# Seventeen of twenty-two up-projection pairs by half products, their weight sums spread over the kernel

## The chip, the cores and the metric

The kernel runs on one core of one Trainium2 chip, as one program in one launch. The metric is the time on the device in microseconds (us); lower is better. Engines are named as the profile names them: PE is the matrix engine (PEld its weight loads), DVE the vector engine, ACT the scalar engine, POOL GpSimd, SP the engine that only issues transfers.

## The reference, cut to what matters

One decoder layer over 512 tokens of width 1024 in float32: two parallel token mixers (RWKV-7 and sparse attention), gated together and projected, then a gated feed-forward part with 2816 channels:

```
x = x + rms_norm(m @ w_out, norm_mix_post)            # x2 in the kernel
h = rms_norm(x, norm_ffn_pre)
u = causal_dwconv(h @ ffn_up, ffn_conv_w, ffn_conv_b)  # width 3 over tokens
u_gate, u_val = split(u, 2)
x = x + rms_norm((silu(u_gate) * u_val) @ ffn_down, norm_ffn_post)
```

## The kernel before, in words

**Precision.** Each float32 operand is split into a high and a low part (`split_to`, L161 on): a 256 KB transfer on SP brings the raw weight tile (L163), ACT copies it to the high part (its call has the helper's line, L129), POOL or DVE subtracts to get the low part (L167). A product is three matmuls: high x high, high x low, low x high.

**Stages.** Norm and projections, the two mixers, two branch projections (`branch`), the output projection (`wo_tok`), the up-projection, the down-projection (`tok_mm`), the last norm and residual (`post`). The mixers are written as generators that a planner (`spawn`, `drive`) steps side by side with a rate each. Within an engine, the framework's scheduler chooses the order at build time; `keep_in_program_order` pins an instruction.

**Up stage.** The 44 blocks of 128 channels form 22 pairs, j = 0 to 21, a gate block and a value block each. A plain pair takes 48 matmuls of 512 tokens, each block into one PSUM bank. Pairs in `SEVEN` go by half products instead (`seven`, L1563 on): the weight pair is taken as a 2 x 2 matrix of quarters (gate or value, half of the 1024 inputs), the normalised tokens as another (half of the inputs, half of the tokens), and seven products of quarters, with additions before and after, replace eight. Each product is 12 matmuls of 256 tokens, 84 for a pair. It needs seven weight tiles a pair, four of them sums of quarters, and four token forms (sums and differences of the token quarters, `forms`). The token forms are made once, by `token_forms`, stepped along with the blocks of pairs 2 to 6 by `next(side)`.

**Weight sums.** The four sums of each pair's quarters are made in DRAM, without an engine's arithmetic: POOL issues copies and adding transfers from the weights to `fsum` (`weight_sums`, L247 the copies, L249 the adds). Ten pairs lie in groups of four, four and two (`SGRP`); each group takes eight transfers, one after the other, 24 in all. The planner steps them at rate 0.06; `run(ws)` ahead of the second branch loop issues what is left.

**Buffers.** PSUM has tags pj, px, py and pz of two banks each. A half-product pair uses two banks for its gate and value (`g`, `v`) and one of pz for a temporary (`t`). Even pairs take both banks of pj, odd ones one of px and one of py. Plain pairs after the first half-product pair take pj for both blocks. Split half-product weights (`form_w`) alternate between pool `wp` (three buffers, shared with plain weights) and pool `sw` (four; three raws). `sw` opens at pair 7, on the right side of SBUF, where the raws of the token forms were. The elementwise tail of a pair (L1624 to L1639) does bias and convolution taps (ACT, two DVE steps for each block), SiLU, the product, and the split of the result into `ah` and `al`.

**Residual.** `x2`, 512 x 1024 floats, stays in SBUF (16 KB a partition) from the output projection to `post`.

Of the kernel before, what the change touches and what calls it, by code (L numbers as in the profile page):

```python
# [13 lines left out]
OP = mybir.AluOpType  # L14
# [10 lines left out]

V_GMIX, V_GFFN, V_MU, V_MUL, V_W0, V_A0, V_KK, V_KA, V_RK, V_LNW, V_LNB = 0, 8, 16, 40, 43, 51, 59, 67, 75, 83, 91
WB = 3
SEVEN = (7, 8, 10, 11, 13, 14, 16, 17, 19, 20)
SGRP = 4
UPOS = {j: i for i, j in enumerate(SEVEN + tuple(sorted(set(range(22)) - set(SEVEN))))}  # L30
RB = 4
WU = 2
# [15 lines left out]
def hybrid_layer(ctx: ExitStack, tc: tile.TileContext, a, out, dbg=None, stop=None):  # L48
# [188 lines left out]
    vd_ = dr.tile([4, 128, S], F32, name="vd_", bufs=1)  # L237
    fsum = [[dr.tile([len(x), 128, 512], F32, name=f"fs{i}{x[0]}", bufs=1) for i in range(4)] for x in SGROUPS]

    def weight_sums():  # L240
        for x, (f1, f2, f3, f4) in zip(SGROUPS, fsum):
            q = [[a["up4"][r, c, UPOS[x[0]]:UPOS[x[-1]] + 1] for c in range(2)] for r in range(2)]
            for o, i, acc in ((f1, q[1][0], None), (f3, q[0][0], None), (f1, q[1][1], OP.add), (f3, q[1][0], OP.add),
                              (f2, f1, None), (f2, q[0][0], OP.add), (f4, f2, None), (f4, q[0][1], OP.add)):
                o, i = (y.rearrange("n (p r) f -> (n p) (r f)", r=4) for y in (o, i))
                if acc is None:
                    tc.keep_in_program_order(po.dma_start(o, i, max_dma_last_dim=8192))  # L247
                else:
                    tc.keep_in_program_order(po.dma_start(o, i, accum_op=acc, max_dma_last_dim=8192))  # L249
                yield  # L250
# [685 lines left out]
    def core(g):  # L936
        return spawn(invert(G[g], g), 0, 1.0), spawn(recur(G[g], g), RD[g], RR[g])

    spawn(ws, 60, 0.06)
    drive(inputs(0, os_[0]), spawn(itertools.chain(compress(0), compress(1)), 0, 0.8))  # L940
    ncx.close()
    rh_ = pool("rh", "right", rhx)
# [387 lines left out]
        split_to(a["wo"][half, q][:, kk * 512:kk * 512 + 512], hi, lo, f"wok{i}", 512, ve if i < NW else po, p, late=i < NW)  # L1330
        wo_w[half, k] = hi, lo

    run(ws)
    with pool("bp", "left") as bp:
        spb = [bp.tile([128, KT, S], F32R, name=f"sp{y}") for y in range(2)]
        load = load_branch(1, obd, spb[0], spb[1], os_[7].acc)
        next(load)
        for _ in fill:
            next(load, None)
        run(load)  # L1340
        second = [branch(1, o8, spb[0], spb[1]) for o8 in range(8)]
# [12 lines left out]
    x2 = fx.tile([128, 4, D], F32, name="x2")
    cvec = fx.tile([128, 176], F32, name="cvec")
    sy.dma_start(cvec, a["cvec"])
    f4ctx = ExitStack()
# [51 lines left out]
        sc.activation(junk, acc, AF.Square, accum_out=ss[:, 0:1])  # L1409
        return ss  # L1410

    def post(acc, res, ss, gb, name, p, t, each):
        junk = p.tile([128, 512], F32, tag=name + "jk", name=f"{name}jl{t}", bufs=2)
        sc.activation(junk, acc, AF.Square, accum_out=ss[:, 1:2])  # L1414
        tm = p.tile([128, 512], F32, tag=name + "tm", name=f"{name}tm{t}", bufs=3)
        ve.tensor_tensor(ss[:, 2:3], ss[:, 0:1], ss[:, 1:2], op=OP.add)  # L1416
        ve.tensor_tensor(tm, acc, gb[:, 512:], op=OP.mult)
        r = rstd_of(ss[:, 2:3], D, f"{name}r{t}", p)
        for i, q in enumerate((res[:, t, :], tm)):
            hs = slice(i * 512, i * 512 + 512)  # L1420
# [69 lines left out]
    after = {NU: split_w(upw(NU), f"up{NU}", True)}  # L1490
    octx.close()
    bctx.close()
    dump("x2", x2.rearrange("p a b -> p (a b)"))


    with pool("ff") as ff:
# [9 lines left out]
            return t[:, r * hf:(r + 1) * hf, (lft, rgt)[c]]  # L1506

        def token_forms():
            with pool("tr", "right") as tr_:
                raws = [{(r, n): tr_.tile([128, 2, 256], F32, tag=f"tr{r}{n}", name=f"tr{c}{r}{n}", bufs=1)  # L1510
                         for r in range(2) for n in range(2)} for c in range(2)]

# [15 lines left out]
                for c in range(2):  # L1528
                    load(c, 0, 1)
                    load(c, 0, 0)  # L1530
                    diff(c, (0, 0), (0, 1), (0, 0))
                    yield
                    high(c, 0, (0, 0))
                    load(c, 1, 1)
                    diff(c, (0, 1), (0, 1), (1, 1))
                    yield
                    high(c, 2, (0, 1))
                    low(c, 0, (0, 0))
                    diff(c, (1, 1), (1, 1), (0, 0))
                    load(c, 1, 0)  # L1540
                    yield
                    high(c, 1, (1, 1))
                    low(c, 2, (0, 1))
                    diff(c, (1, 0), (1, 0), (1, 1))
                    yield
                    high(c, 3, (1, 0))
                    low(c, 1, (1, 1))
                    yield
                    low(c, 3, (1, 0))
            yield  # L1550

        keep = tc.keep_in_program_order
        ring = itertools.count()

        def form_w(src, name, eng):
            n = next(ring)
            p_, tags, b = (wp, ("raw", "whi", "wlo"), WB) if n % 2 else (sw, ("sraw", "shi", "slo"), RB)
            hi = p_.tile([128, 512], F32R, tag=tags[1], name=name + "h", bufs=b)
            lo = p_.tile([128, 512], F32R, tag=tags[2], name=name + "l", bufs=b)
            split_to(src, hi, lo, name, 512, eng, p_, tag=tags[0], bufs=WB)  # L1560
            return hi, lo

        def seven(j):  # L1563
# [16 lines left out]
            def w(i, eng):  # L1580
                return form_w(fs[i - 1] if isinstance(i, int) else a["up4"][i[0], i[1], UPOS[j]], f"sw{j}{i if isinstance(i, int) else 5 + 2 * i[0] + i[1]}", eng)

            g, v, t = (px if j % 2 else pj)(f"sg{j}"), (py if j % 2 else pj)(f"sv{j}"), pz(f"st{j}")
            u2, u4 = (sw.tile([128, 256], F32, tag=f"u{i}", name=f"su{i}{j}", bufs=1) for i in (2, 4))
            prod(g[:, lft], w((0, 0), po), tok(0, 0))
            prod(t[:, lft], w(2, po), forms[1])
# [15 lines left out]
        for j in range(22):  # L1602
            us = []
            sv_ = None
            if j == SEVEN[0]:
                for _ in side:
                    pass
                sw = pool("sw", "right", sctx2)
            if j in SEVEN:
                sv_ = seven(j)  # L1610
            for x in range(2):
# [13 lines left out]
                ve.scalar_tensor_tensor(u[:, 1:], p[:, :S - 1], cvec[:, cv + 1:cv + 2], u[:, 1:], op0=OP.mult, op1=OP.add)  # L1625
                ve.scalar_tensor_tensor(u[:, 2:], p[:, :S - 2], cvec[:, cv:cv + 1], u[:, 2:], op0=OP.mult, op1=OP.add)  # L1626
                us.append(u)
                if 1 < j < SEVEN[0]:
                    next(side, None)
            if sv_ is None:  # L1630
                sc.activation(us[0], us[0], AF.Silu)
                po.tensor_tensor(us[1], us[0], us[1], op=OP.mult)  # L1632
# [10 lines left out]
        with pool("ep") as ep:  # L1643
            g3 = bcast(ep, 3, "gb4")
            res2 = ep.tile([128, 4, 512], F32, name="res2")
            s2 = {}

            def done2(t, acc):
# [114 lines left out]
```

## Time and profile before

| what | value |
|---|---|
| median of 3 runs | 1190.36 us (1188.17 to 1190.53) |
| profiled execution | 1191.81 us, its span 1190.0 us, mean granted clock 0.984 |
| PE busy | 1148.1 us, 96% |
| DVE, ACT, POOL busy | 636.0, 611.4, 578.2 us |
| HBM read, written | 137.13 MB, 40.11 MB |
| up stage starts | 803.56 us from the span's start |
| first half product | 882.34 us |
| first down matmul | 1063.99 us |

A matmul of 512 tokens starts every 0.23 us here, one of 256 tokens every 0.12. Matmuls are pipelined, so the length of one row is more than its distance to the next. Views of the profile quoted below: busy time by stretches (a stretch of time, its length, then busy us and count by engine, the granted clock as a share of full speed, the mean busy share of the 16 DMA engines, GB/s), waits (who waited for whom, us in total, times, longest), groups of instructions (busy us, mean ns | idle before them, and what ended it) and instructions in order of time.

### The profile page before, as it was taken

What the parts mean: (1) busy time and instruction counts of PE and PEld (TensorE: products, weight loads), DVE (VectorE), ACT (ScalarE), POOL (GpSimd) and SP (SyncE); (2) the same over time, 40 slices, a digit from 0 to 9 for tenths busy, and PEclk for the clock granted to TensorE, in tenths of its full rate; (3) what the DMA queues carried; (4) which work ended last, traced back from release to release, by engine and by line L of the source; (5) the groups of instructions that cost most, each with busy time, mean ns of one, the idle gap of its engine ahead of it and who ended that gap; (6) DMA issues with size and microseconds to landing.
All of it is one profiled execution on the core that took longest, in us unless ns stands there. A gap on an engine that the chain in (4) does not pass through costs nothing.

```text
span 1190.0 us, 20753 instructions
## 1 busy us (share of the span) xinstructions
PE 1148.1 (96%) x7698; PEld 934.6 (79%) x7698; DVE 636.0 (53%) x1298; ACT 611.4 (51%) x1206; POOL 578.2 (49%) x554
## 2 busy tenths in 40 slices
PE   9999989999899999999999999999997989989997
PEld 7888877777788787667777778889877988978886
DVE  4236646635565642687887746556745664631103
ACT  5447663544556334576776644444554664533311
POOL 4346754436666453465444335303664665644440
PEclk9999999999999999989999999999998999989999
DMA  6422578633666784244532146711344553324421
GB/s 239 121 75 82 166 161 218 193 117 109 179 173 170 226 229 131 73 115 149 175 125 63 54 142 196 241 36 45 92 134 138 154 155 108 125 92 137 132 66 71
DMA packets 102775, 160.85 MB, mean 135 GB/s; under 512 B 34897, under 2 KB 37777, under 8 KB 99858
## 3 DMA queue, kind: packets, MB, share of 16 engines
q1 hardware_dynamic: 83874, 124.13, 33.8%
q0 software_dynamic: 2944, 20.97, 7.7%
q10 hardware_dynamic: 15856, 14.42, 3.7%
q8 instruction: 61, 1.00, 0.3%
q14 instruction: 40, 0.33, 0.1%
HBM read 137.13 MB, written 40.11 MB: 149 GB/s over the span
## 4 chain that ended last, share of the span: by engine, by line
PE 84%; DVE 4%; DMA 4%; ACT 3%; POOL 2%; issue 2%; SPq 0%; DVEq 0%; POOLq 0%; ACTq 0%
PE sg L1574 4%; PE pu L227 3%; PE pu L228 3%; PE dn L1368 3%; PE dn L1369 3%; PE dn L1370 3%; PE pu L229 3%; PE o L1193 3%; PE st L1574 3%; PE pt L145 3%; PE ub L1251 2%; PE ub L1253 2%; PE ub L1252 2%; PE gt L325 2%; PE gt L327 2%; PE gt L326 2%
## 5 line engine op out<-in xcount | busy, mean ns | idle before, releaser
L1141 ACT ACTIVATE p<-p,stt 128x384 f32<-128x384 f32 (+3 forms) x128 | 70.7, 554 | 32.8 <-DVE stt L1139 32.4
L1139 DVE CUSTOM_DVE_ANT_0 p<-s,rh 128x384 f32<-128x384 f32 (+3 forms) x128 | 59.0, 483 | 22.9 <-PE s L1125 18.9
L1113 POOL TENSOR_SCALAR p<-p,stt 128x512 f32<-128x512 f32 (+1 forms) x64 | 38.9, 623 | 38.5 <-DVE stt L1106 25.2
L1625 DVE SCALAR_TENSOR_TENSOR u<-pu,cvec,u 128x511 f32<-128x511 f32 x24 | 18.0, 749 | 60.6 <-ACT u L1624 60.6
L145 PE MATMUL pt<-ident,p 128*128 128x128 f32 x320 | 44.8, 274 | 1.1 <-DVE p L1115 1.1
L145 PEld LDWEIGHTS pt<-ident,p 128*128 128x128 f32 x320 | 38.1, 141 | 6.2 <-DVE p L1115 1.5
L1132 PE MATMUL s<-kst,qs 128*128 128x512 f32 (+1 forms) x128 | 39.4, 398 | 2.6 <-DVE stt L1139 2.0
L1193 PE MATMUL o<-PT,vt 128*64 128x384 f32 (+3 forms) x256 | 40.6, 443 | 0.0
L1115 DVE TENSOR_SCALAR p<-p,stt 128x512 f32<-128x512 f32 (+1 forms) x64 | 33.1, 544 | 0.7
L1184 ACT ACTIVATE PT<-pt 128x512 f32<-128x512 f32 x48 | 27.4, 586 | 9.9 <-PE pt L145 9.8
L1193 PEld LDWEIGHTS o<-PT,vt 128*64 128x64 f32 x256 | 16.4, 136 | 18.6 <-issue 16.3
L1132 PEld LDWEIGHTS s<-kst,qs 128*128 128x128 f32 x128 | 21.4, 191 | 11.3 <-DVE stt L1139 7.4
L1416 DVE TENSOR_TENSOR p2ss<-p2ss 128x1 f32<-128x1 f32 x4 | 0.6, 160 | 52.1 <-ACT p2jl L1414 52.1
L1186 DVE COPY PT<-pt 128x512 f32<-128x512 f32 x32 | 21.8, 681 | 8.6 <-PE pt L145 8.5
L1141 ACT ACTIVATION_READ_ACCUMULATOR p<-p,stt 128x1 f32 x128 | 24.2, 189 | 0.0
L843 ACT ACTIVATE UV<-xs 64x256 f32<-64x256 f32 x16 | 6.0, 377 | 35.0 <-PE xs L838 34.6
L1639 DVE TENSOR_TENSOR al<-u,ah 128x512 fp32r<-128x512 f32 x12 | 10.8, 897 | 22.8 <-ACT ah L1638 22.7
L691 DVE TENSOR_TENSOR XP<-XP,TM 128x30 f32<-128x30 f32 (+14 forms) x60 | 20.3, 338 | 2.0
L355 DVE SCALAR_TENSOR_TENSOR V<-v,vec,V 128x511 f32<-128x511 f32 x8 | 6.0, 749 | 28.7 <-ACT V L352 28.7
L1632 POOL TENSOR_TENSOR u<-u,u 128x512 f32<-128x512 f32 x12 | 16.3, 1359 | 9.7 <-DVE u L1626 9.7
L631 PE MATMUL g<-AR,KB 64*128 64x128 f32 x256 | 18.0, 295 | 3.0 <-DVE AR L596 3.0
L689 DVE TENSOR_TENSOR TM<-XL,XP 128x30 f32<-128x30 f32 (+14 forms) x60 | 19.6, 326 | 2.0
(2148 smaller groups left out, 4279.3 us busy)
## 6 DMA issues: line engine op xcount, KB each, us to landing
fs<-in_up_dram POOLq DMA_DIRECT2D x12, 1024.0 KB, 9.3
gtd<-gt ACTq DMA_DIRECT2D x16, 256.0 KB, 4.8
fs<-fs POOLq DMA_DIRECT2D x4, 1024.0 KB, 6.2
qs<-qd SPq DMA_DIRECT2D x32, 128.0 KB, 3.3
g<-gtd SPq DMA_DIRECT2D x16, 256.0 KB, 2.9
fs<-in_up_dram POOLq DMA_DIRECT2D x6, 512.0 KB, 5.3
xt<-in_x_dram SPq DMA_DIRECT2D x4, 512.0 KB, 5.3
bvd<-bv SPq DMA_DIRECT2D x8, 256.0 KB, 4.0
```

Of the source, the lines that this page charges most:

```text
L145: return te.transpose(o, i, ident)
L227: te.matmul(p, wh(k), mh(k), start=first and k == 0, stop=False)
L228: te.matmul(p, wh(k), ml(k), start=False, stop=False)
L229: te.matmul(p, wl(k), mh(k), start=False, stop=last and k == n - 1)
L1113: po.tensor_scalar(o.pe[e, b, k], o.pe[e, b, k], w, 1.0, op0=OP.mult, op1=OP.mult)
L1132: m = te.matmul(s_[:, :n], qt, kt[:, x, b, :n], start=x == 0, stop=x == 1)
L1139: ve.tensor_tensor_reduce(sb, parts[b], rh[e][:, (3 - qb) * 128:], -1.0, BIG, OP.add, OP.min, st[e][:, 0, i:i + 1])
L1141: sc.activation(sb, sb, AF.Exp, scale=-1.0, bias=st[e][:, 0, i:i + 1], accum_out=st[e][:, 1, i:i + 1])
L1193: te.matmul(acc[e * 64:e * 64 + 64, j * 128:], vt[:, j, b * 256 + g * 64:b * 256 + g * 64 + 64], m[e][:, c:c + n], start=False, stop=k == ...
L1368: te.matmul(acc[half, t], sh[:, k, tsl], wh[kk], start=k == 0, stop=False)
L1369: te.matmul(acc[half, t], sh[:, k, tsl], wl[kk], start=False, stop=False)
L1574: te.matmul(p, w[y][:, ks], x[z][:, k, :], start=first and k + n == 0, stop=last and k == hf - 1 and n == 2, skip_group_check=True)
```

## The change

All pairs from 5 to 21 go by half products. The sums lie in nine groups of two (the last of one); two groups are stepped alternately, 72 transfers of 512 KB (eight of 256 KB), at rate 0.08, then one for each block of the second branch loop, then one for each up block until none is left. The order of the sums within a group changes (the same sums). The token forms are stepped from pair 0 on, with their raws on the left side; pool `sw` opens at pair 2 and has four raws and five high and low parts, and three of eight forms go to `wp`, five to `sw`. Even and odd pairs change places in PSUM. `x2` is stored to DRAM (`x2d`) by four transfers on SP during the output projection, and loaded again by four on SP behind the up stage.

```diff
-SEVEN = (7, 8, 10, 11, 13, 14, 16, 17, 19, 20)
-SGRP = 4
+SEVEN = (5, 6, 7, 8, 9, 10, 11, 12, 13, 14, 15, 16, 17, 18, 19, 20, 21)
+SGRP = 2
...
+    def group_sums(x, f):
+        q = [[a["up4"][r, c, UPOS[x[0]]:UPOS[x[-1]] + 1] for c in range(2)] for r in range(2)]
+        for o, i, acc in ((0, q[1][0], None), (2, q[0][0], None), (0, q[1][1], OP.add), (2, q[1][0], OP.add),
+                          (1, f[0], None), (1, q[0][0], OP.add), (3, f[1], None), (3, q[0][1], OP.add)):
+            o, i = (y.rearrange("n (p r) f -> (n p) (r f)", r=4) for y in (f[o], i))
+            kw = {} if acc is None else {"accum_op": acc}
+            tc.keep_in_program_order(po.dma_start(o, i, max_dma_last_dim=8192, **kw))
+            yield
+
     def weight_sums():
...
+        gs = [group_sums(x, f) for x, f in zip(SGROUPS, fsum)]
+        for i in range(0, len(gs), 2):
+            for _ in range(8):
+                for y in gs[i:i + 2]:
+                    next(y)
+                    yield
...
-    spawn(ws, 60, 0.06)
+    spawn(ws, 60, 0.08)
...
-    run(ws)
...
             run(second[o8])
+            next(ws, None)
...
     fx = pool("fx", "right", fctx)
-    x2 = fx.tile([128, 4, D], F32, name="x2")
...
     op = pool("op", "left", octx)
+    x2 = op.tile([128, 4, D], F32, name="x2")
+    x2d = dr.tile([4, 128, D], F32, name="x2d", bufs=1)
...
         xn[t] = norm_x(x2[:, t, :], t, [g2b[:, 0:512], g2b[:, 512:]], "n2", op)
+        sy.dma_start(x2d[t], x2[:, t, :])
...
-            with pool("tr", "right") as tr_:
+            with pool("tr", "left") as tr_:
...
-            n = next(ring)
-            p_, tags, b = (wp, ("raw", "whi", "wlo"), WB) if n % 2 else (sw, ("sraw", "shi", "slo"), RB)
...
+            n = next(ring) % 8
+            p_, tags, b = (wp, ("raw", "whi", "wlo"), (WB, WB)) if n % 3 == 1 else (sw, ("sraw", "shi", "slo"), (4, 5))
...
-            g, v, t = (px if j % 2 else pj)(f"sg{j}"), (py if j % 2 else pj)(f"sv{j}"), pz(f"st{j}")
+            g, v, t = (pj if j % 2 else px)(f"sg{j}"), (pj if j % 2 else py)(f"sv{j}"), pz(f"st{j}")
...
+            if j == 2:
+                sw = pool("sw", "right", sctx2)
             if j == SEVEN[0]:
                 for _ in side:
                     pass
-                sw = pool("sw", "right", sctx2)
...
-                if 1 < j < SEVEN[0]:
+                if j < SEVEN[0]:
                     next(side, None)
+                next(ws, None)
...
             res2 = ep.tile([128, 4, 512], F32, name="res2")
+            x2 = ep.tile([128, 4, D], F32, name="x2b")
+            for t in range(4):
+                sy.dma_start(x2[:, t, :], x2d[t])
```

More of the change, by code (lines that the diff above doesn't have):

```diff
@@ L238, in hybrid_layer @@
     fsum = [[dr.tile([len(x), 128, 512], F32, name=f"fs{i}{x[0]}", bufs=1) for i in range(4)] for x in SGROUPS]
-    def weight_sums():
[L241 to L250, printed above, removed]
+    def group_sums(x, f):
[6 more added lines that the diff above has]
+            yield
+    def weight_sums():
+        gs = [group_sums(x, f) for x, f in zip(SGROUPS, fsum)]
[4 more added lines that the diff above has]
+                    yield
     gates = con.tile([128, 4, 48], F32, name="gates")
@@ L1410, in stat, with post @@
         return ss
-    def post(acc, res, ss, gb, name, p, t, each):
+    def post(acc, res, ss, gb, name, p, t, each, x2):
         junk = p.tile([128, 512], F32, tag=name + "jk", name=f"{name}jl{t}", bufs=2)
@@ L1492, in hybrid_layer @@
     bctx.close()
-    dump("x2", x2.rearrange("p a b -> p (a b)"))
     with pool("ff") as ff:
@@ L1547, in token_forms @@
                     low(c, 1, (1, 1))
+                    low(c, 3, (1, 0))
                     yield
-                    low(c, 3, (1, 0))
             yield
@@ L1555, in form_w @@
         def form_w(src, name, eng):
-            n = next(ring)
-            p_, tags, b = (wp, ("raw", "whi", "wlo"), WB) if n % 2 else (sw, ("sraw", "shi", "slo"), RB)
-            hi = p_.tile([128, 512], F32R, tag=tags[1], name=name + "h", bufs=b)
-            lo = p_.tile([128, 512], F32R, tag=tags[2], name=name + "l", bufs=b)
-            split_to(src, hi, lo, name, 512, eng, p_, tag=tags[0], bufs=WB)
+            n = next(ring) % 8
+            p_, tags, b = (wp, ("raw", "whi", "wlo"), (WB, WB)) if n % 3 == 1 else (sw, ("sraw", "shi", "slo"), (4, 5))
+            hi = p_.tile([128, 512], F32R, tag=tags[1], name=name + "h", bufs=b[1])
+            lo = p_.tile([128, 512], F32R, tag=tags[2], name=name + "l", bufs=b[1])
+            split_to(src, hi, lo, name, 512, eng, p_, tag=tags[0], bufs=b[0])
             return hi, lo
@@ L1659, in hybrid_layer @@
             for t in range(4):
-                post(part(t), res2, s2[t], g3, "p2", ep, t, store)
+                post(part(t), res2, s2[t], g3, "p2", ep, t, store, x2)
     fctx.close()
```

## The prediction, made before the result was known

> **What bounds the kernel now.** I read the page first, then busy time by stretches of the up stage, then the waits of TensorE there, then the operations of a half-product pair.
>
> ```profile
> span 1190.0 us, 20753 instructions
> ...
> PE 1148.1 (96%) x7698; PEld 934.6 (79%) x7698; DVE 636.0 (53%) x1298; ACT 611.4 (51%) x1206; POOL 578.2 (49%) x554
> ...
> PE 84%; DVE 4%; DMA 4%; ACT 3%; POOL 2%; issue 2%; SPq 0%; DVEq 0%; POOLq 0%; ACTq 0%
> ```
>
> TensorE is the bound, so what shortens its queue, or its waits, shortens the kernel. The profiled execution took 1191.81 us, 1.8 more than its span and 1.45 above the median of 1190.36. The change acts on the up stage. Its stretch from pair 5 to the first down matmul, cut where the kind of pair changes (columns: stretch and length; busy PE, PEld, DVE, ACT, POOL; granted clock, DMA share, GB/s):
>
> ```profile
> 860.60:882.34 21.74, 21.74 (x98) 18.00 (x97) 11.16 (x15) 12.10 (x21) 13.85 (x11) 1.00 0.37 107
> 882.34:928.20 45.86, 37.02 (x219) 33.36 (x218) 22.80 (x34) 21.58 (x38) 22.62 (x17) 0.85 0.46 144
> 928.20:948.16 19.96, 19.92 (x169) 19.75 (x169) 13.20 (x22) 13.46 (x24) 15.30 (x11) 1.00 0.50 148
> 948.16:959.06 10.90, 10.90 (x50) 9.01 (x50) 6.25 (x10) 5.59 (x9) 5.18 (x4) 1.00 0.54 167
> 959.06:978.90 19.84, 19.64 (x169) 19.43 (x167) 13.23 (x23) 13.57 (x24) 15.52 (x11) 1.00 0.52 151
> 978.90:995.92 17.02, 12.76 (x50) 10.43 (x51) 5.96 (x9) 5.54 (x10) 5.15 (x4) 0.90 0.32 104
> 995.92:1015.88 19.96, 19.92 (x169) 19.75 (x169) 13.10 (x22) 13.46 (x24) 15.21 (x11) 1.00 0.52 147
> 1015.88:1026.78 10.90, 10.90 (x50) 9.01 (x50) 6.16 (x10) 5.72 (x10) 5.19 (x4) 1.00 0.51 167
> 1026.78:1045.00 18.22, 18.22 (x159) 18.22 (x158) 11.20 (x19) 10.16 (x18) 11.95 (x9) 1.00 0.29 86
> 1045.00:1063.99 18.99, 14.70 (x61) 11.96 (x60) 6.55 (x10) 6.39 (x10) 5.73 (x5) 0.82 0.31 99
> sum 203.39, PE 185.73 PEld 168.93 DVE 109.60 ACT 107.57 POOL 115.70; mean PE 18.57 PEld 16.89 DVE 10.96 ACT 10.76 POOL 11.57
> ```
>
> Two plain pairs take 21.74 us (10.87 each), two half-product pairs 19.96 (9.98 each): a converted pair is worth only 0.89 us. But 7 plain and 10 half-product pairs at these prices make 7 x 10.87 + 10 x 9.98 = 175.9 us, and the stretch took 203.39: 27.5 us are lost, 17.7 of them idle (203.39 - 185.73), the rest at a lower clock. Who is waited for, from the first up matmul on:
>
> ```profile
> PE pu L227 <- DVE sv L1637: 13.8, 3, 5.0
> PE sg L1574 <- ACT su L1587: 1.1, 1, 1.1
> PE sv L1574 <- ACT sw81h L129: 1.0, 1, 1.0
> PE sg L1574 <- POOL sw85l L167: 1.0, 1, 1.0
> PE sg L1574 <- ACT sw85h L129: 0.8, 1, 0.8
> ```
>
> Three waits of a plain pair's first matmul (L227) carry 13.8 us. In the code, plain pairs after pair 6 take both buffers of the PSUM tag pj, and an even half-product pair holds both of them until its last elementwise step. Plain pairs 9, 15 and 21 come right behind the even pairs 8, 14 and 20; 12 and 18 come behind odd ones, which use px and py, and wait for nothing (10.90 us stretches). The other four waits, 3.9 us, lie at the first half-product pairs.
>
> What a wait leaves behind (start, length, matmul):
>
> ```profile
> 892.41 0.41 PE L1574 MATMUL sg<-hl,sw75h 128*128 128x256 f32 x1
> 895.28 0.28 PE L1574 MATMUL st<-tf2h,sw73h 128*128 128x256 f32 x1
> ...
> 915.29 0.76 PE L227 MATMUL pu<-hh,up18h 128*128 128x512 f32 x1 [5.03 <-DVE sv L1637]
> 918.41 0.63 PE L228 MATMUL pu<-hl,up18h 128*128 128x512 f32 x1
> ...
> 919.15 0.40 PE L227 MATMUL pu<-hh,up18h 128*128 128x512 f32 x1
> ```
>
> After the wait of 5.03 us matmuls run at 0.63 instead of 0.40 us for some 3.5 us, until 919. At 892 they run at 0.41 instead of 0.28 although no gap before was over 1.0 us. [...]
>
> **The change, part by part.**
>
> *Pairs 5 to 21 all by half products.* Seven pairs x 0.89 = -6.2 us. No plain pair follows a half-product pair any more, so the three pj waits go with their tails. Who is late next on PSUM? Odd pairs now take both pj, even ones px and py, so a pair meets its own banks two pairs later. The wait at 915.29 ended about 5 us behind the last product of pair 8; the pair between lasts 9.98: cover of about 5 us. With nothing late, 17 x 9.98 = 169.7 us instead of 203.4: **-33.7 us**. The rest is what comes back.
>
> *Can the other engines hold 9.98 us a pair without plain pairs between?* Operations of half-product pairs (busy and mean ns), then L167 (low-part subtracts: DVE, POOL) and L129 (ACT) alone in the two-pair stretch:
>
> ```profile
> L1625 DVE SCALAR_TENSOR_TENSOR u<-sg,cvec,u 128x511 f32<-128x511 f32 x10 | 7.4, 743 | 4.2 <-ACT u L1624 4.2
> ...
> L1624 ACT ACTIVATE u<-sv,cvec 128x512 f32<-128x512 f32 x10 | 7.8, 779 | 7.4 <-DVE sv L1578 7.4
> ...
> L1578 DVE TENSOR_TENSOR sv<-st,su 128x256 f32<-128x256 f32 x20 | 8.5, 424 | 0.7 <-PE st L1574 0.3
> ...
> L1639 DVE TENSOR_TENSOR al<-sv,ah 128x512 fp32r<-128x512 f32 x10 | 6.9, 691 | 3.4 <-ACT ah L1638 3.3
> L1637 DVE TENSOR_TENSOR sv<-u,sg 128x512 f32<-128x512 f32 x10 | 6.9, 691 | 0.5
> ...
> L1635 ACT ACTIVATE sg<-u 128x512 f32<-128x512 f32 x10 | 6.0, 602 | 0.0
> ...
> 928.20:948.16 19.96, 3.27 (x4) 14.10 (x10) 1.00 0.50 148
> ...
> 928.20:948.16 19.96, 8.62 (x15) 1.00 0.50 148
> ```
>
> DVE: 2 subtracts x 0.82 + 5 adds x 0.42 + 4 x 0.74 + 2 x 0.69 = 8.1 us. ACT: 7 high parts x 0.57 + 2 x 0.78 + three copies of about 0.6 = 7.4. POOL: 5 x 1.41 = 7.1. All are under 9.98, the tightest (DVE) by 1.9. In the stretch shown TensorE was busy 19.92 of 19.96 with the second pair running beside the first one's elementwise tail, and ACT made 15 high parts, more than two pairs' 14. The deeper rings help: weight forms go to 3 + 5 buffers instead of 3 + 3 usable by strict alternation, eight products or 11.4 us ahead. For 17 pairs I allow 0 (this stretch) to 1.1 us (the single wait on su) each and take 3 us, nearer the stretch that repeated three times.
>
> *Start of the half products.* Pairs 7 and 8 ran badly: the stretch 882.34 to 928.20 holds them and plain pair 9, ideal 30.8, lost 15.0; the wait on pj and its tail (5.0 + 8 matmuls x 0.23) are 6.9 of that, so the start cost about 8. Their weights' pool opened only when the token forms were done; now it opens at pair 2, on the other side from the forms' raws, and the forms start at pair 0 instead of 2. They have five plain pairs as before (DVE 11.2 of 21.7 us busy in two). Bounds 0 and 8; I take 3, as POOL must fill the ring beside plain pairs and sums.
>
> *Weight sums.* 72 transfers instead of 24:
>
> ```profile
> q0 software_dynamic: 2944, 20.97, 7.7%
> ...
> fs<-in_up_dram POOLq DMA_DIRECT2D x12, 1024.0 KB, 9.3
> ...
> fs<-in_up_dram POOLq DMA_DIRECT2D x6, 512.0 KB, 5.3
> ...
> x<-in_x_dram SPq DMA_DIRECT2D x4, 512.0 KB, 6.4
> ...
> L249 POOL DMA_DIRECT2D fs<-in_up_dram x12: 777/832/1162, 146.4 to 507.5; - x12
> L247 POOL DMA_DIRECT2D fs<-in_up_dram x6: 537/560/756, 120.2 to 405.3; - x6
> ...
> 765.00:770.00 5.00, 5.00 (x23) 4.14 (x23) 0.31 (x1) 0.61 (x2) 0.00 (x0) 1.00 1.02 399
> ```
>
> An issue holds POOL 0.56 us (copy) or 0.83 (add): 0.7 on the mean. At rate 0.06 the 24 spanned 400 of the planner's steps by 507.5 us; counted through the loops there are 461, and 0.08 x 461 gives 36 transfers in the mixers, 8 in the second branch loop, 28 in blocks 0 to 27, that is pairs 0 to 13. After block 3 the sums of pairs 13 to 16 are complete, after pair 9 those of 17 to 20, after pair 13 those of pair 21: none is late. In the mixers the bytes fall (36 x 0.52 = 18.9 MB for 20.97) and POOL issues 12 x 0.7 = 8.4 us more. Bounds 0 and 8.4 (all of it on the path); POOL carries 2% of the chain, so I take 0.5.
>
> In pairs 5 to 9 two sums of 0.52 MB meet seven loads (1.84 MB). By the shares, loads cost 0.50 x 19.96 us at 148 GB/s = 3.4 us per MB, 6.2 us a pair; the sums, 7.7% of 1190 us for 20.97 MB = 4.4 us per MB, 4.6 us. Together 10.8 us of DMA in 9.98: 0.8 too much in five pairs, 4 us; in pairs 10 to 13 the sums halve and it fits. Bounds: 0 (loads alone moved 399 GB/s in 765 to 770, and both together ask for 290) and 18 (below). I take 4.
>
> *POOL's queue.* A dependent sum waits on POOL for its predecessor to land (5.3 us for 512 KB, 9.3 for 1024), and the five subtracts of a pair queue behind it, then TensorE. Two groups alternate, so within the up stage a predecessor is one pair (9.98 us) older; only the last group follows itself.
>
> *x2 in DRAM.* Four stores of 512 KB on SP in the output projection sit ahead of the first up weights, needed 15 us and more later; x2 of a tile is ready before the next tile's 10.9 us of matmuls ends. I take 0; the upper bound is one landing exposed, 6.4 us. Four loads come back when the half-product buffers fall free, as pair 21 ends, ahead of later down weights on SP: 2.1 MB at 399 GB/s is 5.3 us of DMA beside 99 GB/s (last stretch of the table). Bounds 0 and 5.3; I take 1.5, since two to three down weights (2.7 us of matmuls each) are loaded by then.
>
> Sum: -33.7 + 3 + 3 + 0.5 + 4 + 1.5 = **-21.7 us**; 1191.8 becomes 1170.1, and against the median **1169 us**.
>
> **The rivals.**
>
> *Nothing comes back.* The stretch at 9.98 a pair repeats 17 times: -33.7, 1157 us. For it: three such stretches. Against: each had a plain pair before it, and no sums.
>
> *The sums take the place of the stalls.* Adding transfers beside seven loads land in 9.3 instead of 5.3 us, POOL stands up to 2 us for each pair's predecessors and the splits come late: 9 pairs x 2 = 18 instead of 4: 1183 us. For it: POOL's 7.1 + 1.4 us is 85% of a pair already. [...] Against: the distance of a whole pair between dependent sums.
>
> *The plain pairs were the refill.* Pairs 7 and 8, without plain pair 9 and its wait:
>
> ```profile
> 882.34:909.97 27.63, 23.83 (x168) 22.72 (x167) 15.77 (x25) 15.68 (x28) 17.03 (x13) 0.88 0.55 171
> ```
>
> That is 13.8 us each. If POOL and ACT can only restore the ring beside plain pairs, 17 x 13.8 = 235 us instead of 203: **1222 us, slower**. It decides from 203.4 / 17 = 11.96 us a pair upwards. Against: 15 high parts in 19.96 us.
>
> *Stalls only move*, and the half products give their 6.2 us at most: 1184 to 1190.
>
> **How the numbers follow.** Forecast (1160 to 1177) 0.52; nothing comes back 0.15; sums hold POOL 0.17; stalls move 0.08, half of it within 0.2% (2.4 us, about what a measurement here can tell from no change); refill 0.08. Faster 0.52 + 0.15 + 0.17 + 0.04 = 0.88, same 0.04, slower 0.08. The range 1156 to 1184 takes in the first three and leaves out some 0.16.
>
> **What would show it.** L227 waits on L1637 gone; pairs of half products 9.98 to 10.4 us apart, 10.5 to 11 in pairs 5 to 9; the granted clock 1.00 over the stretch; POOL's waits on landings short; first down matmul near 1042. The prediction is wrong if sv or sg products wait for POOL's low parts in pair after pair, if x2's loads hold SP before the first down weights, or if the deeper rings were no help because high parts wait for ACT.

## The result, and the profile after

The changed kernel takes **1173.85 us** in the median (1171.43 to 1175.2) beside 1190.44 for the kernel before on the same chip: ratio 0.985, 95% interval 0.982 to 0.988. The forecast was 1169, its own range 1160 to 1177, the whole range 1156 to 1184. Line numbers move a little: the products are L1581 now, the additions behind them L1585, the elementwise tail L1632 to L1648, the sums' issues L246.

The head of the page:

```profile
span 1173.4 us, 21515 instructions
...
PE 1133.0 (97%) x7950; PEld 931.5 (79%) x7950; DVE 675.9 (58%) x1354; ACT 624.1 (53%) x1234; POOL 602.1 (51%) x602
```

The span fell by 16.6 us, TensorE's busy time by 15.1. Busy time by stretches, from the first up matmul to the end: blocks 0 to 2, the rest of the five plain pairs, then half-product pairs 5, 6, 7, 8, 9, 10, 11, 12 to 20 together, 21, and the down-projection and last norm.

```profile
801.20:820.10 18.90, 18.90 (x162) 18.76 (x161) 15.15 (x20) 7.29 (x16) 5.31 (x5) 1.00 0.37 126
820.10:866.90 46.80, 41.66 (x171) 33.38 (x170) 37.45 (x38) 25.88 (x43) 31.02 (x29) 0.93 0.70 198
866.90:882.30 15.40, 11.57 (x85) 11.38 (x84) 8.12 (x11) 6.83 (x12) 10.31 (x9) 0.89 0.76 187
882.30:892.10 9.80, 9.80 (x87) 9.80 (x86) 7.30 (x14) 6.94 (x13) 8.03 (x9) 1.00 0.79 282
892.10:901.90 9.80, 9.80 (x87) 9.80 (x86) 6.62 (x13) 5.71 (x11) 7.65 (x7) 1.00 0.96 251
901.90:913.50 11.60, 9.97 (x86) 9.77 (x86) 8.77 (x14) 8.06 (x14) 8.12 (x10) 1.00 0.81 283
913.50:923.20 9.70, 9.70 (x86) 9.70 (x85) 6.59 (x13) 5.05 (x10) 6.45 (x6) 1.00 0.97 234
923.20:940.00 16.80, 12.91 (x87) 12.71 (x86) 9.43 (x14) 8.64 (x15) 9.86 (x10) 0.80 0.58 206
940.00:949.80 9.80, 9.80 (x87) 9.80 (x86) 7.29 (x14) 6.89 (x12) 7.54 (x7) 1.00 0.79 209
949.80:1037.40 87.60, 87.60 (x759) 87.60 (x758) 65.02 (x118) 62.56 (x109) 61.92 (x48) 1.00 0.66 199
1037.40:1047.05 9.65, 9.65 (x87) 9.65 (x85) 5.99 (x12) 4.74 (x8) 3.88 (x3) 1.00 0.18 57
1047.05:1173.40 126.35, 119.87 (x530) 98.95 (x528) 21.97 (x39) 35.43 (x66) 42.63 (x33) 0.99 0.36 119
```

Three things are to be seen. The pace that repeats is 9.73 us a pair (87.60 / 9), with TensorE never idle. Against it pairs 5, 8 and 10 lose 5.7, 1.9 and 7.1 us, while sums are still under way (DMA share up to 0.97). And the plain pairs 0 to 4 take 18.90 + 46.80 = 65.7 us, where before they took 860.60 - 803.56 = 57.0. The account of the span:

| stretch | before | after | difference |
|---|---|---|---|
| start to first up matmul | 803.56 | 801.20 | -2.4 |
| plain pairs 0 to 4 | 57.0 | 65.7 | +8.7 |
| pairs 5 to 21 | 203.4 | 180.1 | -23.3 |
| first down matmul to end | 126.0 | 126.35 | +0.35 |

Who TensorE waits for, from the up stage on:

```profile
PE st L1581 <- DVE su L1585: 9.3, 3, 3.9
PE pu L227 <- ACT up5h L129: 3.6, 1, 3.6
PE pu L229 <- POOL up9l L167: 1.6, 1, 1.6
```

The 13.8 us of waits on pj (`L227` for `L1637` before) are gone, as forecast. In their place stand three waits on `su`, in pairs 5, 8 and 10, and two in the plain pairs. What lies behind the third wait on `su`, in pair 10 (ACT and DVE, then TensorE: start, length, instruction, idle time before it and what ended it):

```profile
925.12 0.63 ACT L129 ACTIVATE sw104h<-sw104r 128x512 fp32r<-128x512 f32 x1 [5.29 <-DMA sw104r<-fs]
925.65 0.61 ACT L129 ACTIVATE sw108h<-sw108r 128x512 fp32r<-128x512 f32 x1
...
926.30 1.37 DVE L167 TENSOR_TENSOR sw108l<-sw108r,sw108h 128x512 fp32r<-128x512 f32 x1 [3.80 <-ACT sw108h L129]
```

```profile
927.27 0.28 PE L1581 MATMUL sv<-tf0h,sw101l 128*128 128x256 f32 x1
931.45 0.58 PE L1581 MATMUL st<-tf2h,sw103h 128*128 128x256 f32 x1 [3.89 <-DVE su L1585]
...
936.31 0.41 PE L1581 MATMUL sg<-hl,sw106h 128*128 128x256 f32 x1
```

ACT stands 5.29 us for one load of 256 KB, `sw104r`, which took 11.4 us to land. The high part behind it, `sw108h`, is late by that; DVE stands 3.80 us for its low part, the tail of pair 9 and the addition `su` are queued behind that on DVE, and TensorE waits 3.89 us for `su`. Then matmuls take 0.41 instead of 0.28 us for over 5 us, which is the rest of the pair's 7.1. The wait in pair 8, 1.63 us, has another late load behind it (chain of waits: start, length, what):

```profile
894.36 8.14 DMA sw88r<-in_up_dram
```

The same load took 2.6 us in a run without sums beside it (e2 below; KB, then us from issue to landing):

```profile
sw88r<-in_up_dram SPq DMA_DIRECT2D x1, 256.0 KB, 2.6
```

The wait in pair 5, the second largest, is of another kind:

```profile
871.34 0.63 ACT L129 ACTIVATE sw65h<-sw65r 128x512 fp32r<-128x512 f32 x1 [4.98 <-PE sv L1581]
...
875.06 0.38 PE L1581 MATMUL st<-tf2h,sw53h 128*128 128x256 f32 x1 [3.83 <-DVE su L1585]
```

The first high part of pair 6, `sw65h`, stands at the head of ACT's queue for 4.98 us until TensorE ends pair 5's product `sv` (871.24), which is read here as the wait for a buffer of the weights' ring. Its own load, 6.8 us in flight, landed in the same moment (871.23), so either alone would have held it as long. Behind it on ACT stand the tail of the last plain block and the copy `su` of pair 5, and TensorE waits 3.83 us for what DVE makes of them.

### The profile page after: what moved, and what is told of

Same layout as the page of the kernel before. It is cut to its first block, busy times and chain, and to the rows that moved or that the text cites. A ratio compares the mean times of both kernels' runs of the same rounds, so it can differ in the third digit from the quotient of the medians.

```text
span 1173.4 us, 21515 instructions
## 1 busy us (share of the span) xinstructions
PE 1133.0 (97%) x7950; PEld 931.5 (79%) x7950; DVE 675.9 (58%) x1354; ACT 624.1 (53%) x1234; POOL 602.1 (51%) x602
## 4 chain that ended last, share of the span: by engine, by line
PE 54%; DMA 6%; DVE 6%; ACT 2%; issue 2%; POOL 2%; SPq 0%; DVEq 0%; POOLq 0%; ACTq 0%
PE sg L1581 6%; PE st L1581 5%; PE dn L1374 3%; PE dn L1373 3%; PE dn L1375 3%; PE o L1199 3%; PE pt L145 2%; PE ub L1257 2%; PE sv L1581 2%; PE ub L1259 1%; PE ub L1258 1%; PE q L331 1%; PE s L1138 1%; PE q L333 1%; PE q L332 1%
## 5 line engine op out<-in xcount | busy, mean ns | idle before, releaser
L1147 ACT ACTIVATE p<-p,stt 128x384 f32<-128x384 f32 (+3 forms) x128 | 70.7, 555 | 37.1 <-DVE stt L1145 36.8
L1145 DVE CUSTOM_DVE_ANT_0 p<-s,rh 128x384 f32<-128x384 f32 (+3 forms) x128 | 59.2, 484 | 19.6 <-PE s L1131 16.4
L246 POOL DMA_DIRECT2D fs<-in_up_dram x54 | 38.9, 743 | 4.5 <-DMA fs<-fs 4.3
L1190 ACT ACTIVATE PT<-pt 128x512 f32<-128x512 f32 x48 | 27.4, 586 | 10.4 <-PE pt L145 10.2
L1585 DVE TENSOR_TENSOR sg<-sg,su 128x256 f32<-128x256 f32 x17 | 7.4, 433 | 37.1 <-PE sg L1581 37.1
L1447 PE MATMUL wo<-woh,mh 128*128 128x512 f32 x52 | 21.1, 405 | 0.5 <-ACT mh L1267 0.5
L1449 PE MATMUL wo<-woh,ml 128*128 128x512 f32 x52 | 21.1, 406 | 0.0
L1448 PE MATMUL wo<-wol,mh 128*128 128x512 f32 x52 | 20.9, 402 | 0.0
```

What stands on the lines that cost most here:

```text
L1145: ve.tensor_tensor_reduce(sb, parts[b], rh[e][:, (3 - qb) * 128:], -1.0, BIG, OP.add, OP.min, st[e][:, 0, i:i + 1])
L1147: sc.activation(sb, sb, AF.Exp, scale=-1.0, bias=st[e][:, 0, i:i + 1], accum_out=st[e][:, 1, i:i + 1])
```

## The experiments

Two losses were to be explained: the stretch of half-product pairs (180.1 where 17 x 9.73 = 165.4 would do), and the plain pairs (+8.7). All kernels are the changed one with the edit shown, except where the kernel before is named.

**e1_sums_early: all sums in the mixers.**

```diff
-    spawn(ws, 60, 0.08)
+    spawn(ws, 60, 0.16)
```

> The changed kernel with the planner's rate for the weight sums at 0.16 instead of 0.08, so that all 72 end in the mixers. Theory T (the sums' DMA traffic in the up stage costs the 11 us that pairs 5 to 11 lost beyond 9.75 us each): the stretch from the first half product to the first down matmul falls from 180.1 to 166 to 170 us; the mixers get twice the sums and lose 0 to 8 us; total 1160 to 1172 us. Rival (the losses come from the start itself and from the order of work): the stretch stays at 177 to 181 us, total 1173 or more.

Measured: 1165.25 us, ratio to the kernel before 0.977 [0.973, 0.981]. The stretch is free of any loss, 165.40 us with TensorE busy in all of it; the up stage starts 9.6 us later (810.79), so the mixers pay for part of what the stretch gains. How much is rough: each trace is of one execution, and in the traces of the changed kernel and of e2 to e5, whose code ahead of the up stage is the same, that stage starts at 795.6 to 802.0.

```profile
875.03:1040.43 165.40, 165.40 (x1429) 165.40 (x1428) 119.98 (x216) 115.65 (x200) 113.50 (x84) 1.00 0.58 178
```

**e2_no_up_sums: the 28 transfers of the up stage left out** (the products of later pairs read plain quarters in place of sums).

```diff
+                if isinstance(i, int) and n >= 8:
+                    return form_w(a["up4"][r_, c_, UPOS[j]], f"sw{j}{i}", eng)
...
-                next(ws, None)
```

> The changed kernel without the 28 sums of the up stage (left out: the half products of pairs 13 to 21 read plain quarters in their place, same loads in number and size). Everything ahead of the up stage is as in the changed kernel. Theory T: the waits on su at pairs 6, 9 and 11 go, pairs 6 to 21 run at 9.7 to 9.8 us, the stretch of half products falls from 180 to 166 to 170 us, total 1160 to 1164 us. Rival (weights are late because the start leaves the ring empty): at least two of the three waits stay, stretch 176 to 181, total 1170 to 1174.

Measured: 1158.91 us, ratio 0.973 [0.968, 0.978]. The stretch is again 165.40:

```profile
859.56:1024.96 165.40, 165.40 (x1429) 165.40 (x1428) 119.98 (x216) 115.67 (x200) 113.45 (x84) 1.00 0.57 177
```

Two different ways of taking the sums out of the up stage give one number. So the 14.7 us (180.1 - 165.4), the start at pair 5 included, are what 28 transfers in the up stage cost. Not all of it is shown to be late loads: the framework also orders the work otherwise here. POOL's first low part of pair 5 begins 27.7 us behind the first up matmul in e1 and e2, 50.2 in the changed kernel. The plain pairs stay at 63.9, so their loss is mostly not the sums'. Their longest wait in e1 and e2 is 3.1 us, at block 5 like the 3.6 of the changed kernel, but for POOL's low part `up5l`, not for ACT.

**e3_small_up_sums: the same 28 issues with a sixteenth of the bytes** (so the sums of later pairs are incomplete, and quarters are read instead).

```diff
+            if up_stage:
+                o, i = o[:, 0:128], i[:, 0:128]
```

> The changed kernel with the 28 sums of the up stage cut to a sixteenth of their bytes, each still issued and waited for by POOL (the half products of pairs 13 to 21 read plain quarters). If the price is DMA bytes: as without the sums, 1160 to 1165 us. If it is POOL, which issues them and waits for predecessors with the subtracts queued behind: as the changed kernel, 1170 to 1174 us, and the waits on su stay.

Measured: 1171.43 us, ratio 0.983 [0.980, 0.985], as slow as the full sums in total, but not in the same places (plain pairs, then the stretch):

```profile
799.75:869.02 69.27, 61.17 (x330) 51.64 (x328) 50.51 (x58) 33.08 (x60) 40.36 (x35) 0.95 0.36 105
869.02:1039.31 170.29, 167.32 (x1429) 167.12 (x1428) 125.08 (x216) 115.92 (x200) 123.38 (x100) 0.99 0.56 175
```

The waits in pairs 5, 8 and 10 are all gone, so the 14.7 us went with the bytes (and the order: POOL's first low part of pair 5 comes at 28.9 us here). The 4.9 us that the stretch loses are new and lie in pairs 12 and 13, where the changed kernel lost nothing. A subtract of DVE took 5.69 us beside five subtracts of POOL (940.56 to 947.04; such a step takes 0.69 alone), and TensorE waited 2.97 us for the addition behind it:

```profile
941.91 5.69 DVE L167 TENSOR_TENSOR sw131l<-sw131r,sw131h 128x512 fp32r<-128x512 f32 x1
...
948.59 0.39 PE L1585 MATMUL st<-tf3h,sw128h 128*128 128x256 f32 x1 [2.97 <-DVE sv L1589]
```

The plain pairs got worse by 3.6 though the DMA share fell from 0.6 to 0.36: they don't wait for bandwidth. No theory on record was met in total; by place, the theory of bytes holds for the stretch.

**e4_forms_late: the token forms stepped along pairs 2 to 4**, two steps a block in pairs 2 and 3.

```diff
-                if j < SEVEN[0]:
+                if 1 < j < SEVEN[0]:
                     next(side, None)
+                    if j < 4:
+                        next(side, None)
```

> The changed kernel with the token forms stepped along pairs 2 to 4 (two steps a block in pairs 2 and 3) instead of pairs 0 to 4. Theory F (the wait of 3.6 us before block 5 and its low clock, 8.7 us lost in the plain pairs, come from DVE's token forms in pairs 0 and 1, which delay the elementwise tail and with it ACT's queue): the plain pairs fall from 65.7 to 57 to 60 us; the half products may start up to 4 us later; total 1165 to 1171. Rival W (half-product weights taken up in ACT's queue ahead of plain ones): the wait before block 4 or 5 stays, total 1172 to 1178.

Measured: 1175.66 us, ratio 0.986 [0.985, 0.988]; plain pairs 70.7, worse by 5. The wait at block 5 is gone, and others stand at block 6 (3.1 us, ACT's `up6h`) and block 9 (5.8, POOL's `up9l`). But the edit moved only the later steps of the forms: DVE still makes the first six ahead of the first elementwise tail, 10.2 to 18.2 us behind the first up matmul as in the changed kernel. So whether these six cost the plain pairs was not tested.

**e5_weights_late: pool `sw` opened at pair 4 instead of 2.**

```diff
-            if j == 2:
+            if j == 4:
                 sw = pool("sw", "right", sctx2)
```

> The changed kernel with the pool of the half-product weights opened at pair 4 instead of pair 2. Theory W (subtracts and high parts of pair 5's weights stand ahead of those of blocks 4 to 6 in POOL's and ACT's queues): blocks 4 to 6 run at 5.45 us each, the plain pairs take 57 to 60 us instead of 65.7; the first half products wait 0 to 5 us more; total 1165 to 1173. Rival (token forms alone, or sums): the wait before block 5 or 6 stays and the total is 1173 to 1178.

Measured: 1173.24 us, ratio 0.985 [0.982, 0.987], no change. The edit did not do what it was for: ACT still took four parts of pair 5's weights ahead of those of block 5, and the wait of 3.6 us stayed. Nothing follows for the theories.

**e6_before_x2: the kernel before with only `x2` through DRAM.**

```diff
-    x2 = fx.tile([128, 4, D], F32, name="x2")
+    x2 = op.tile([128, 4, D], F32, name="x2")
+    x2d = dr.tile([4, 128, D], F32, name="x2d", bufs=1)
...
+        sy.dma_start(x2d[t], x2[:, t, :])
...
+            x2 = ep.tile([128, 4, D], F32, name="x2b")
+            for t in range(4):
+                sy.dma_start(x2[:, t, :], x2d[t])
```

> The kernel before with x2's way through DRAM alone (four stores in the output projection, four loads behind the up stage). Theory: nothing of it is on the path, the time stays at 1188 to 1193 us. Rival: the stores hold SP ahead of the first up weights, or the loads hold the down weights: 1194 to 1200.

Measured: 1189.78 us, ratio 1.000 [0.998, 1.003]: free. In the changed kernel the loads take 7.4 us to land (KB each, then us from issue to landing), and the down stage is 0.35 us longer:

```profile
x2b<-x2d SPq DMA_DIRECT2D x4, 512.0 KB, 7.4
```

**e7_before_banks: the kernel before with one line changed**, so that the plain pairs 9, 15 and 21 take banks that are free.

```diff
-                    p = ((pj, px, py, pz)[blk % 4] if j < SEVEN[0] else pj)(f"pu{blk}")
+                    p = ((pj, px, py, pz)[blk % 4] if j < SEVEN[0] else pj if j in (12, 18) else (px, py)[x])(f"pu{blk}")
```

> The kernel before with one line changed: plain pairs 9, 15 and 21 take px and py instead of both buffers of pj, so that they no longer wait for the elementwise tail of the even pair ahead. Theory (the three waits of 13.8 us and their low clock were PSUM buffers, nothing else): 13.8 + 3 x 1.9 less, 1169 to 1174 us. Rival (weights or DVE are late as well, the wait moves): a wait of 2 us or more on ACT or POOL stands in each place, 1178 to 1190.

Measured: 1167.49 us, ratio 0.980 [0.977, 0.983]: 23 us, more than the whole change, and a little below the 1169 to 1174 us that were expected. Among TensorE's waits in its up stage there is none of L227 on L1637 any more, and the longest is:

```profile
PE sg L1574 <- ACT su L1587: 1.8, 1, 1.8
```

So what was lost before at pairs 9, 15 and 21 was a choice of banks, and could be had back without another half product. The stalls did not move on to other waits.

**e8_sums_mid: rate 0.11**, 50 of 72 transfers in the mixers instead of 36.

```diff
-    spawn(ws, 60, 0.08)
+    spawn(ws, 60, 0.11)
```

> The changed kernel with the planner's rate at 0.11: 50 sums in the mixers, 8 in the second branches, 14 in pairs 0 to 6. The stretch of half products falls from 180 to 166 to 172 us as without sums; the mixers lose less than the 9.6 us of rate 0.16, 1 to 6 us; total 1160 to 1168 us. Rival: mixers and up stage give in total what the sums cost anywhere, 1166 to 1174.

Measured: **1157.6 us**, ratio 0.972 [0.969, 0.975], 16 us under the changed kernel. The up stage starts at 797.29, no later than with the slower rate, and after pair 7 no pair loses anything (plain pairs; pairs 5 to 7; pairs 8 to 21):

```profile
797.29:861.25 63.96, 59.82 (x329) 50.92 (x328) 49.75 (x55) 29.91 (x55) 35.28 (x31) 0.97 0.56 163
861.25:895.19 33.94, 30.54 (x253) 29.87 (x252) 26.05 (x40) 23.34 (x41) 27.24 (x23) 1.00 0.70 201
895.19:1031.35 136.16, 136.16 (x1178) 136.16 (x1177) 99.86 (x181) 95.11 (x165) 91.67 (x68) 1.00 0.57 178
```

What the sums cost depends on where they lie: little with 50 in the mixers, some 9.6 us there with all of them, 14.7 in the stretch with 28 left for the up stage.

**e9_mid_pinned: e8 with ACT's high parts of pair 5's weights held behind the plain pairs.**

```diff
-        def form_w(src, name, eng):
+        def form_w(src, name, eng, late=False):
...
+                split_to(src, hi, lo, name, 512, eng, p_, late, tags[0], b[0])
...
+                return form_w(..., eng, j == SEVEN[0])
```

> The kernel with rate 0.11, and ACT's high parts of the first half-product pair pinned to their place behind the plain pairs, so that four of them no longer stand ahead of block 5's on ACT. Theory W (they are what block 5 waits for): the wait of 3.6 us and its low clock go, blocks 3 to 9 run at 5.45 us; the start of pair 5 loses some of that, as seven high parts come at once: total 1152 to 1160 us. Rival (ACT and DVE are late there anyway, through the token forms): the wait before block 5 or 6 stays at 2 us or more, total 1157 to 1164.

Measured: 1170.91 us, ratio 0.984 [0.981, 0.987], 13 us worse than e8. Waits of TensorE:

```profile
PE sg L1581 <- ACT sw55h L129: 5.5, 1, 5.5
PE pu L229 <- POOL up5l L167: 3.9, 1, 3.9
...
PE pu L227 <- ACT up5h L129: 1.4, 1, 1.4
```

The wait at block 5 for ACT fell from 3.6 to 1.4 us, and POOL's low part of the same block became late instead, for 3.9. So ACT's order was one of two waits in line there. The weights of pair 5 are missing at its start (5.5), and pairs 5 and 6 take 13.4 and 16.4 us. Pair 6, 6.7 us over the pace, has a cause of its own: a subtract of DVE that took 6.53 us beside five of POOL (875.75 to 882.04), as in e3; TensorE waited 3.5 us for an addition behind it.

```profile
876.07 6.53 DVE L167 TENSOR_TENSOR sw61l<-sw61r,sw61h 128x512 fp32r<-128x512 f32 x1
```

**e10_mid_pinned_forms: e9 and the late forms of e4.**

> The same with the token forms stepped along pairs 2 to 4 as well. If DVE's token forms in pairs 0 and 1 delay the first elementwise tails, and through them ACT's queue, blocks 3 to 5 lose nothing now: 5.45 us each; then pair 5 is later, for forms and weights come close together. Total 1152 to 1162 us. If it is the weights alone, no better than with the forms early.

Measured: 1172.92 us, ratio 0.986 [0.983, 0.990]; the wait for `sw55h` is 8.9 us. Worse than e8 as well. As in e4, DVE still makes the first six steps of the forms ahead of the first tail, so the theory of the forms was not tested here either.

**e11_big_sums: groups of four, 40 transfers of up to 1 MB**, the same bytes for the planner's step.

```diff
-SGRP = 2
+SGRP = 4
...
-    spawn(ws, 60, 0.08)
+    spawn(ws, 60, 0.055)
```

> The changed kernel with groups of four pairs, 40 transfers of 1 MB (the last eight 256 KB) at rate 0.055, so that the mixers move the same 26 MB as with rate 0.11 in half the transfers; the rest falls in the second branches and pairs 0 to 3. If the price of a sum is bytes: as with rate 0.11, 1154 to 1161 us. If it is the transfer (its issue, its landing): 2 to 5 us less. If large transfers hold the engines' queues longer against the mixers' small ones: 2 to 8 us more.

Measured: 1177.91 us, ratio 0.990 [0.986, 0.994]. The stretch is better than with 512 KB (166.7 us), but the stages ahead of it are longer: the first branch matmul 597.17 (588.02 in e8), the first up matmul 822.24 (797.29). Its profiled execution was the slowest of the five (1183.6). In its chain of waits a weight of the output projection is in flight for 12.81 us:

```profile
764.37 12.81 DMA wok15r<-in_wo_dram
```

POOL had issued two adding transfers at that moment (its instructions in order of time):

```profile
764.30 1.32 POOL L246 DMA_DIRECT2D fs<-in_up_dram  x2
```

TensorE waits 6.6 us behind it, for the high part `mh` of ACT. The larger transfers, up to 1 MB where e8 has 512 KB, made the time longer, 1177.9 for 1157.6 us at the same bytes for a step. The load that was late is shown; that nothing else made the other stages longer is not.

**e12_from_seven: e8 with pairs 5 and 6 plain again.**

```diff
-SEVEN = (5, 6, 7, 8, 9, 10, 11, 12, 13, 14, 15, 16, 17, 18, 19, 20, 21)
+SEVEN = (7, 8, 9, 10, 11, 12, 13, 14, 15, 16, 17, 18, 19, 20, 21)
```

> The version with the sums at rate 0.11, with pairs 5 and 6 plain again: half products run from pair 7 to 21, seven plain pairs ahead of them; the token forms still begin with pair 0, the pool of the half products' weights still opens at pair 2, and 51 of the 64 transfers still lie in the mixers. Two pairs more by plain products cost 2 x (10.88 - 9.75) = 2.3 us. In the version at 0.11 the five plain pairs took 64.0 us where 5 x 10.88 = 54.4 would do (9.6 lost) and pairs 5 to 7 lost 13.3 + 10.0 + 10.7 - 29.3 = 4.7. Theory C (crowding: forms, half-product weights and plain weights together are too much for ACT, DVE and POOL in five plain pairs, and seven dilute it): the seven plain pairs take 78 to 81 us (76.2 without loss), the first three half-product pairs 30 to 31; about 8 to 11 us gained for 2.3 paid, 1149 to 1153 us. Theory P (place: the loss is a fixed price of the order in which the engines take the forms and the weights at blocks 5 to 9, wherever the half products begin): the same 9.6 lost, seven plain pairs 85 to 87 us, and 1158 to 1161 us; a wait of 3 to 4 us at block 5 on a high part of ACT stays.

Measured: 1156.74 us, ratio 0.972 [0.969, 0.975], not to be told from e8. Seven plain pairs, then fifteen by half products:

```profile
792.27:882.21 89.94, 83.28 (x425) 70.14 (x424) 56.08 (x69) 43.49 (x76) 48.68 (x39) 0.96 0.43 126
882.21:1028.55 146.34, 146.32 (x1261) 146.11 (x1260) 107.44 (x189) 101.43 (x175) 98.16 (x74) 1.00 0.57 175
```

The half products start without loss (146.34 / 15 = 9.76), as crowding would have it; but the plain pairs lose more than either theory allows, 11.2 us against the 78.8 that the seven plain pairs took in the kernel before (803.56 to 882.34), with the wait of 3.6 at block 5 as before. Neither theory is met whole. The loss up to the steady pace is about the same in both: 11.2 here; in e8 6.9 in the plain pairs (64.0 - 57.0) and 4.7 in pairs 5 to 7 (33.94 - 3 x 9.73).

## Why the prediction was right, and where it was not

The sign, the size within its range, and the main mechanism were right: no plain pair follows a half-product pair, the waits on pj and their tails go, and e7 shows that these were worth 23 us alone. That the total came within 5 us of the forecast is in part luck: the stretch with nothing late was 7.3 us better than its two terms, and that pays for nearly half of the 16.4 us that the sums, the start and the plain pairs cost beyond theirs. By the steps of the sum:

| step | forecast | measured | by |
|---|---|---|---|
| stretch with nothing late | -33.7, then +3 for small waits | -38.0 (165.4 for 203.4) | e1, e2 |
| start of half products, and the sums in pairs 5 to 9 | +3 +4 | +14.7 | 180.1 - 165.4 (5.7 in pair 5, 9.0 in pairs 8 and 10) |
| plain pairs 0 to 4 | 0 | +8.7 | 65.7 - 57.0 |
| mixers and branches to the up stage | +0.5 | -2.4 | 801.20 - 803.56, within the spread told under e1 |
| x2 through DRAM | +1.5 | +0.35, free alone | table, e6 |
| sum | -21.7 | -16.6 | |

Of the signs that it named, L227's waits are gone. The pace of 9.73 us lies below the 9.98 to 10.4; the clock over the stretch was 0.97, not 1.00; pairs 5 to 9 took 9.7 to 15.4 us, not 10.5 to 11; the first down matmul came at 1047.05, not near 1042.

*The pace.* 9.98 us was the mean of two pairs, the first of which came right behind a plain pair. Without plain pairs between it is 9.73 (165.4 / 17, e1 and e2), and DVE, the busiest engine beside TensorE, holds it with 7.1 us a pair (119.98 / 17). The allowance of 3 us was not needed. Two small readings were off without touching the sum: of ACT's three copies `su` takes 0.37 us, not 0.6, and even pairs, with two buffers each of px and py, meet their own banks four pairs later, not two.

*The sums* were the mis-sized term. I counted DMA time as if it spread evenly: 10.8 us of work in 9.98, so 0.8 a pair. In pairs 8 and 10 what counted was the landing of single loads, 8.1 and 11.4 us where the same two took 2.6 and 3.2 in e2, at a DMA share of 0.96 and 0.97. In pair 10 one late weight held ACT (5.29 us), then DVE's queue (3.80), then TensorE (3.89), and behind that wait the granted clock was 0.50 for some 6 us. In pair 5 (the term for the start, 3) the deeper rings, which I counted as a help, did not keep ACT from standing for a buffer and a load: close to one of the signs of being wrong that I had named, though in one place only. The bound of 18 that I gave for POOL standing for its predecessors had the right size by another way: POOL itself waited 4.3 us for landings in the whole kernel (last column):

```profile
L246 POOL DMA_DIRECT2D fs<-in_up_dram x54 | 38.9, 743 | 4.5 <-DMA fs<-fs 4.3
```

So the rival "the sums take the place of the stalls" named a real price and, in the changed kernel, the wrong holder of it, POOL. In e3 and e9 one DVE subtract beside five of POOL's (5.69 and 6.53 us) did hold a pair; in the half-product pairs of the changed kernel no low part of DVE took more than 1.72 us. That too many sums in the mixers are dear (e1, the up stage some 9.6 us later) did not enter the forecast; its rate costs nothing yet.

*The plain pairs* are the step that failed. "They have five plain pairs as before" took their cover as given, from DVE's 11.2 busy us in two pairs. But pool `sw` opening at pair 2 puts pair 5's weights on ACT among the plain pairs' own, and DVE makes the forms at the same time. ACT's first SiLU of the up stage (its table load is the row) begins 15.9 us behind the first up matmul in the kernel before, 19.7 in the changed kernel, where six steps of the forms stand on DVE ahead of the tail that it waits for. Before:

```profile
819.42 1.28 ACT L1631 ACT_TABLE_LOAD   x1 [1.64 <-DVE u L1626]
```

After (DVE's last four steps of the six, ACT's first SiLU, and the first of four high parts of pair 5 that ACT makes ahead of block 5's), and what TensorE's clock did behind the wait:

```profile
814.83 4.59 DVE L1526 TENSOR_TENSOR tr<-tr,tr 128x512 f32<-128x512 f32 x4
...
820.94 1.28 ACT L1640 ACT_TABLE_LOAD   x1 [5.52 <-DVE u L1634]
...
828.11 0.61 ACT L129 ACTIVATE sw55h<-sw55r 128x512 fp32r<-128x512 f32 x1
```

```profile
832.56 0.79 PE L227 MATMUL pu<-hh,up5h 128*128 128x512 f32 x1 [3.57 <-ACT up5h L129]
...
837.84 0.63 PE L229 MATMUL pu<-hh,up5l 128*128 128x512 f32 x1
839.14 0.40 PE L227 MATMUL pu<-hh,up5h 128*128 128x512 f32 x1
```

The wait is 3.57 us and the low clock after it lasts until 839. Holding ACT's part back (e9), the later steps of the forms (e4), or both (e10) did not help, and two plain pairs more (e12) moved the price. In every run of the changed kernel the six early steps of the forms stay where they are, and ACT's first SiLU is 3.2 us or more later than before, about the length of the wait at block 5; a run without them there is missing, so that they are the cause is not shown. What is shown is that in no run did the two kinds of preparation together come cheaper than some 7 us (e1, e2: plain pairs 64.2 and 63.9 for 57.0, and then no loss), and that they cost 12 in e8 and e12 and more in e4, e9 and e10; which order of ACT, DVE and POOL would hide them is open. The trace of before had a like price in another place, the 8 us that the prediction read at pairs 7 and 8.

*The other rivals.* "Nothing comes back" (1157) is the time that e8 and e12 reach at another rate of sums, but by other terms: the better pace and less time ahead of the up stage pay there for what the plain pairs lose. "The plain pairs were the refill" falls: in nine pairs on end nothing is late. "Stalls only move" falls with e7.

## What to carry to other kernels

Ask of a change that removes a wait whether the wait can be had for less: the one line of bank choice in e7 was worth 23 us, more than the whole change with its seven more half-product pairs. When background transfers are spread over a kernel, don't add up DMA time; look for the stage in which a single late load has the least slack, and set their rate so that few are left for it (here 1157.6 us at 0.11 for 1173.85 at 0.08 and 1165.25 at 0.16). Cover that worked for one kind of preparation is not cover for two at once. And see in the trace whether an edit moved what it was to move: e4, e5 and e10 left in place what they were to hold back, or part of it.

## What the runs showed of the hardware

A DVE subtract with both inputs in SBUF stood for as long as POOL's subtracts followed each other without a gap (DVE, then POOL, start and length, in the changed kernel):

```profile
824.23 0.68 DVE L1532 TENSOR_TENSOR tf0l<-tr,tf0h 128x512 fp32r<-128x512 f32 x1
...
850.91 4.78 DVE L1532 TENSOR_TENSOR tf0l<-tr,tf0h 128x512 fp32r<-128x512 f32 x1
```

```profile
850.10 1.30 POOL L167 TENSOR_TENSOR up8l<-up80r,up8h 128x512 fp32r<-128x512 f32 x1
851.36 1.29 POOL L167 TENSOR_TENSOR sw55l<-sw55r,sw55h 128x512 fp32r<-128x512 f32 x1
852.62 1.27 POOL L167 TENSOR_TENSOR sw53l<-sw53r,sw53h 128x512 fp32r<-128x512 f32 x1
853.86 1.28 POOL L167 TENSOR_TENSOR up8l<-up81r,up8h 128x512 fp32r<-128x512 f32 x1
```

It began inside the first of the four and ended 0.55 us behind the last, 4.78 us where the same step took 0.68 with no subtract of POOL beside it. In the half-product pairs of e3 and e9 one such subtract stood for five of POOL's (5.69 and 6.53 us); TensorE waited 3.0 and 3.5 us behind it, and the stretch lost 4.9 and pair 6 6.7 us with the low clock. The row above lies among the plain pairs; how much of their loss such blocks make was not measured.

The low clock: behind the wait of 3.57 us in the plain pairs the granted clock was 0.50 for 6.1 us (832.56 to 838.67), behind the one of 3.89 in pair 10 it was 0.50 for 6.15 (931.45 to 937.60), so each of these two cost nearly twice its length (half of some 6 us, an estimate, on top of the wait). A wait of 3.57 us in e8 was followed by it for under 4 us. Waits of 3.12 us (e2, block 5: matmuls of 0.63 us for 5 us) and 2.97 us (e3: a granted clock of 0.60 in the 2.4 us behind it) were followed by it too; behind one of 2.60 us (e8, pair 5) and the one of 1.63 us in pair 8 the granted clock stayed at 1.00. The length of one wait does not sort all of them: in the kernel before it was 0.50 in 888.60 to 895.10, behind gaps of 0.98 us at most. What sets it off was not shown.
